# Rotary embedding on one core: from float16 halves on one software queue to float32 pieces on two hardware queues, with the additions on GpSimd

## The chip, the core and the metric

The kernel runs on one NeuronCore of a Trainium2 chip. A core has five instruction streams that matter here: TensorE (unused in this kernel), VectorE (DVE in the profile), ScalarE (ACT), GpSimd (POOL) and SyncE (SP). They run independently and meet through semaphores. SBUF is the on-chip working memory of 128 partitions, PSUM a second and smaller on-chip memory, and HBM the memory outside. Sixteen DMA engines move data between HBM and SBUF; an engine's queue (SP, ACT or POOL) issues a transfer, and the sixteen engines carry it out. A transfer issued by POOL appears in the profile as "software" queue, one issued by SP or ACT as "hardware" queue.

The metric is the device time of the program in microseconds, as the median of several runs. A profiled execution has its own time, and a span, which is the stretch that the trace covers.

## The reference

```python
def setup_inputs():
    batch, seq_len, num_heads, head_dim = (8, 2048, 16, 64)
    return {'x': ..., 'cos': ..., 'sin': ...}    # x [8, 2048, 16, 64], cos and sin [2048, 32], float32

def reference(x, cos, sin):
    x1 = x[..., :head_dim // 2]
    x2 = x[..., head_dim // 2:]
    out1 = x1 * cos - x2 * sin
    out2 = x1 * sin + x2 * cos
    return np.concatenate([out1, out2], axis=-1).astype(np.float32)
```

cos and sin are broadcast over the batch and the heads. The input is 67.1 MB and so is the output. For one element there are two products and one addition: the element times cos, the other half's element times sin (with a minus for the first half), and their sum.

## The kernel before

**Tiling.** The 2048 positions are spread over 128 partitions, so that each partition holds J = 16 consecutive positions ("rows" below); a row is 16 heads of 64 numbers, 1024 elements. One batch is thus a tile of 128 partitions by 16384 elements. All of it is computed in float16: the transfer that loads x converts from float32 to float16 on its way, the one that stores converts back.

**Memory.** `buf` holds five batches in float16 (`NBUF = 5`), batch b in slot b % 5. `v` is one temporary of a batch's size. The tables `cos_h` and `sin_h` are float16 in SBUF; `sin_h` holds minus sin for the first half of a head and sin for the second.

**Arithmetic.** `rotate` (L83 to L100) issues three VectorE instructions for a batch, or for some rows of it: L92 writes `v` as the swapped halves of x times `sin_h`; L98 multiplies `buf` by `cos_h` in place; L100 adds `v` into `buf`. The halves are swapped by reading with a negative step, at no extra instruction.

**Queues.** All large transfers, six loads (L71) and eight stores (L81), are issued by POOL. `in_ring` chains them so that POOL issues them in the order in which they are written. SP loads the tables (L40, L45) and the first two rows of the first batch as float32 (`head`, L41), which ACT converts (L106), and at the end SP stores the last two rows (L135), which ACT has converted back (L134). ACT also makes the float16 tables (L104, L105, L110).

**Order.** Loads of batches 0 and 1 are issued first; then the first two rows are rotated and a row of them is stored; loads of batches 2 to 4 follow; batches 0 to 2 are rotated and stored one by one; loads of batches 5 to 7 wait for the stores that free their slots; then batches 3 and 4, 5 and 6, and 7.

Of the kernel before, what the change touches and what calls it, by code (L numbers as in the profile page):

```python
# [1 line left out]

# [4 lines left out]


@with_exitstack  # L10
def kernel(
    ctx: ExitStack,
    tc: tile.TileContext,
    x: bass.AP,
    cos: bass.AP,
    sin: bass.AP,
    out: bass.AP,
):
    nc = tc.nc
    f16 = mybir.dt.float16  # L20
    f32 = mybir.dt.float32

    B, S, H, D = x.shape
    Dh = D // 2
    P = nc.NUM_PARTITIONS
    J = S // P
    NBUF = 5

    const_pool = ctx.enter_context(tc.tile_pool(name="rope_const", bufs=1))
    io_pool = ctx.enter_context(tc.tile_pool(name="rope_io", bufs=1))  # L30
    tmp_pool = ctx.enter_context(tc.tile_pool(name="rope_tmp", bufs=1))

    JA = 2
    head = const_pool.tile([P, JA, H, D], f32)
    x0 = x[0].rearrange("(p j) h d -> p j (h d)", j=J)
    sin_f = const_pool.tile([P, J, Dh], f32)
    cos_f = const_pool.tile([P, J, Dh], f32)
    cos_h = const_pool.tile([P, J, Dh], f16)
    sin_h = const_pool.tile([P, J, D], f16)
    nc.sync.dma_start(out=sin_f, in_=sin.rearrange("(p j) d -> p j d", j=J))  # L40
    nc.sync.dma_start(  # L41
        out=head.rearrange("p j h d -> p (j h d)"),
        in_=x0[:, 0:JA, :].rearrange("p j f -> p (j f)"),
    )
    nc.sync.dma_start(out=cos_f, in_=cos.rearrange("(p j) d -> p j d", j=J))  # L45

    buf = io_pool.tile([P, NBUF, J, H, D], f16)

    ring = []

    def in_ring(dma):
        if ring:
            tc.add_manual_dep(
                dma.ins,
                ring[-1].ins.name,
                mybir.DependencyInfo(mybir.DependencyClass.NoSync, mybir.DependencyReason.DATA),
                reason="order of the ring",
            )
        ring.append(dma)
        return dma  # L60

    def load(b, n=1):
        k = b % NBUF
        if n == 1:
            j0 = JA if b == 0 else 0
            dst = buf[:, k, j0:J, :, :].rearrange("p j h d -> p (j h d)")
            src = x[b].rearrange("(p j) h d -> p j (h d)", j=J)[:, j0:J, :].rearrange("p j f -> p (j f)")
        else:
            dst = buf[:, k : k + n, :, :, :].rearrange("p b j h d -> p b (j h d)")
            src = x[b : b + n].rearrange("b (p j) h d -> p b (j h d)", j=J)  # L70
        in_ring(nc.gpsimd.dma_start(out=dst, in_=src))  # L71

    def store(b, n=1, j0=0, j1=J):
        k = b % NBUF
        if n == 1:
            src = buf[:, k, j0:j1, :, :].rearrange("p j h d -> p (j h d)")
            dst = out[b].rearrange("(p j) h d -> p j (h d)", j=J)[:, j0:j1, :].rearrange("p j f -> p (j f)")
        else:
            src = buf[:, k : k + n, :, :, :].rearrange("p b j h d -> p b (j h d)")
            dst = out[b : b + n].rearrange("b (p j) h d -> p b (j h d)", j=J)  # L80
        return in_ring(nc.gpsimd.dma_start(out=dst, in_=src))  # L81

    def rotate(b, j0=0, j1=J):  # L83
        v = tmp_pool.tile([P, J, H, D], f16)
        n = j1 - j0
        js = slice(j0, j1)
        xt = buf[:, b % NBUF, js, :, :]
        shape = [P, n, H, 2, Dh]
        sin_b = sin_h[:, js, :].rearrange("p j (e d) -> p j e d", e=2).unsqueeze(2).to_broadcast(shape)
        cos_b = cos_h[:, js, :].unsqueeze(2).to_broadcast([P, n, 2 * H, Dh])  # L90
        xe = xt.rearrange("p j h (e d) -> p j h e d", e=2)
        nc.vector.tensor_mul(  # L92
            out=v[:, js, :, :].rearrange("p j h (e d) -> p j h e d", e=2),
            in0=xe[:, :, :, ::-1, :],
            in1=sin_b,
        )
        xw = xt.rearrange("p j h (e d) -> p j (h e) d", d=Dh)
        nc.vector.tensor_mul(out=xw, in0=xw, in1=cos_b)  # L98
        xa = xt.rearrange("p j h d -> p (j h d)")
        nc.vector.tensor_add(out=xa, in0=xa, in1=v[:, js, :, :].rearrange("p j h d -> p (j h d)"))  # L100

    load(0)
    load(1)
    nc.scalar.copy(out=sin_h[:, :, Dh:D], in_=sin_f)  # L104
    nc.scalar.mul(out=sin_h[:, :, 0:Dh], in_=sin_f, mul=-1.0)  # L105
    nc.scalar.copy(  # L106
        out=buf[:, 0, 0:JA, :, :].rearrange("p j h d -> p (j h d)"),
        in_=head.rearrange("p j h d -> p (j h d)"),
    )
    nc.scalar.copy(out=cos_h, in_=cos_f)  # L110
    rotate(0, 0, JA)
    store(0, 1, 0, 1)
    load(2, 2)
    load(4)
    rotate(0, JA, J)
    store(0, 1, 1, J)
    rotate(1)
    store(1)
    rotate(2)
    store(2)  # L120
    load(5, 2)
    load(7)
    rotate(3)
    rotate(4)
    store(3, 2)
    rotate(5)
    rotate(6)
    store(5, 2)
    rotate(7)
    gate = store(7, 1, 0, 9)  # L130
    store(7, 1, 9, J - JA)
    last = buf[:, 7 % NBUF, J - JA : J, :, :].rearrange("p j h d -> p (j h d)")
    dst = out[B - 1].rearrange("(p j) h d -> p j (h d)", j=J)[:, J - JA : J, :].rearrange("p j f -> p (j f)")
    nc.scalar.copy(out=head.rearrange("p j h d -> p (j h d)"), in_=last)  # L134
    end = nc.sync.dma_start(out=dst, in_=head.rearrange("p j h d -> p (j h d)"))  # L135
    tc.add_manual_dep(
        end.ins,
        gate.ins.name,
        mybir.DependencyInfo(mybir.DependencyClass.Sync, mybir.DependencyReason.DATA),
        reason="the last rows go out behind this part",  # L140
    )


# [1 line left out]
_INS = ['x', 'cos', 'sin']  # L145
_OUTS = [((8, 2048, 16, 64), 'float32')]


# [23 lines left out]
```

## Time and profile before

| what | value |
|---|---|
| median of 3 runs | 316.41 us (316.35 to 316.66) |
| the profiled execution | 316.6 us |
| its span | 314.8 us |
| VectorE busy | 209.1 us in 27 instructions |
| ScalarE busy | 6.8 us |
| GpSimd busy | 8.6 us, in 14 issues of transfers and 4 small memsets |
| HBM read, written | 67.63 MB, 67.11 MB |

The profiled execution takes 1.8 us more than its span. A line of the profile that names a tile or a source line gives, in this order, the line, the engine, the operation, output and inputs, the shapes, how many there were, the busy time in all and the mean of one in ns, and the idle time of that engine just before with what ended it. A line of the timeline begins with the start in us from the span's start, and the duration.

### The profile page before, as it was taken

To read this page: it belongs to the slowest core of one execution; us is meant where nothing else is said; L and a number is where in the kernel's file an instruction comes from. 1 tells how busy PE (TensorE), PEld (TensorE's weight loads), DVE (VectorE), ACT (ScalarE), POOL (GpSimd) and SP (SyncE) were. 2 spreads that over 40 slices of the span, in tenths; PEclk is the share of its full clock that TensorE was granted. 3 is DMA by queue.
4 is the path that set the end of the run, shared out by engine and by line. 5 is a ranking of instruction groups with operands and counts; after the bars stand their busy time and mean duration, and the time that the engine had idled before them with its cause. 6 is when DMAs were issued, how large, how long until landed. Compare 5 with 4: busy or idle time off the path is not lost.

```text
span 314.8 us, 115 instructions
## 1 busy us (share of the span) xinstructions
DVE 209.1 (66%) x27; ACT 6.8 (2%) x6; POOL 8.6 (3%) x18
## 2 busy tenths in 40 slices
DVE  0105999999499999999950000899999999910000
ACT  3200000000000000000000000000000000020000
POOL 1002000000000000000010000000000000010000
DMA  9899999999999899999999999999999999999998
GB/s 284 187 262 200 200 266 200 200 262 204 200 200 317 382 492 407 400 400 533 400 200 208 258 200 200 229 237 333 400 491 441 400 400 525 408 400 400 433 427 339
DMA packets 3104, 101.71 MB, mean 323 GB/s; under 512 B 288, under 2 KB 288, under 8 KB 672
## 3 DMA queue, kind: packets, MB, share of 16 engines
q0 software_dynamic: 2528, 99.09, 98.1%
q1 hardware_dynamic: 576, 2.62, 2.2%
HBM read 67.63 MB, written 67.11 MB: 428 GB/s over the span
## 4 chain that ended last, share of the span: by engine, by line
DVE 66%; another core or an unknown queue 13%; DMA 8%; ACT 1%; issue 0%; SPq 0%; DVEq 0%; ACTq 0%
DVE buf L98 22%; DVE buf L100 22%; DVE v L92 22%; DMA cos_f<-in_cos_dram 8%; ACT head L134 1%; ACT cos_h L110 0%; SPq L41 0%; SPq L40 0%; DVEq L92 0%; ACTq L134 0%
## 5 line engine op out<-in xcount | busy, mean ns | idle before, releaser
L92 DVE TENSOR_TENSOR v<-buf,sin_h 128x16384 f16<-128x16384 f16 (+2 forms) x9 | 69.7, 7744 | 51.4 <-DMA buf<-in_x_dram 41.2
L98 DVE TENSOR_TENSOR buf<-buf,cos_h 128x16384 f16<-128x16384 f16 (+2 forms) x9 | 69.7, 7744 | 15.8 <-ACT cos_h L110 15.5
L100 DVE TENSOR_TENSOR buf<-buf,v 128x16384 f16<-128x16384 f16 (+2 forms) x9 | 69.7, 7744 | 0.3
L81 POOL DMA_DIRECT2D out_dram<-buf x8 | 4.7, 586 | 219.4 <-DVE buf L100 219.4
L134 ACT CAST head<-buf 128x2048 f32<-128x2048 f16 x1 | 1.9, 1898 | 249.9 <-DVE buf L100 249.9
L71 POOL DMA_DIRECT2D buf<-in_x_dram x6 | 3.7, 628 | 49.7 <-DMA out_dram<-buf 48.9
L106 ACT CAST buf<-head 128x2048 f16<-128x2048 f32 x1 | 1.9, 1897 | 3.5 <-DMA head<-in_x_dram 3.5
L104 ACT ACT_TABLE_LOAD x1 | 1.3, 1283 | 0.7 <-PEq L156 0.7
L110 ACT CAST cos_h<-cos_f 128x512 f16<-128x512 f32 x1 | 0.6, 617 | 16.1 <-DMA cos_f<-in_cos_dram 16.1
L104 ACT CAST sin_h<-sin_f 128x512 f16<-128x512 f32 x1 | 0.6, 617 | 1.4 <-DMA sin_f<-in_sin_dram 1.4
L105 ACT ACTIVATE sin_h<-sin_f 128x512 f16<-128x512 f32 x1 | 0.6, 624 | 0.0
L156 POOL MEMSET const-float32-0.0<- 128x1 f32 x1 | 0.1, 100 | 0.2 <-issue 0.2
L156 POOL MEMSET const-bfloat16-1.0<- 128x1 bf16 x1 | 0.1, 103 | 0.0
L156 POOL MEMSET const-float32-1.0<- 128x1 f32 x1 | 0.1, 100 | 0.0
L156 POOL MEMSET const-uint8-127<- 128x1 uint8 x1 | 0.1, 100 | 0.0
## 6 DMA issues: line engine op xcount, KB each, us to landing
buf<-in_x_dram POOLq DMA_DIRECT2D x2, 8192.0 KB, 55.2
buf<-in_x_dram POOLq DMA_DIRECT2D x3, 4096.0 KB, 57.4
out_dram<-buf POOLq DMA_DIRECT2D x1, 7680.0 KB, 68.3
out_dram<-buf POOLq DMA_DIRECT2D x1, 4608.0 KB, 28.6
buf<-in_x_dram POOLq DMA_DIRECT2D x1, 3584.0 KB, 22.3
out_dram<-buf POOLq DMA_DIRECT2D x1, 2560.0 KB, 34.1
head<-in_x_dram SPq DMA_DIRECT2D x1, 1024.0 KB, 6.9
out_dram<-head SPq DMA_DIRECT2D x1, 1024.0 KB, 8.4
```

Of the source, the lines that this page charges most:

```text
L71: in_ring(nc.gpsimd.dma_start(out=dst, in_=src))
L81: return in_ring(nc.gpsimd.dma_start(out=dst, in_=src))
L92: nc.vector.tensor_mul(out=v[:, js, :, :].rearrange("p j h (e d) -> p j h e d", e=2), in0=xe[:, :, :, ::-1, :], in1=sin_b,)
L98: nc.vector.tensor_mul(out=xw, in0=xw, in1=cos_b)
L100: nc.vector.tensor_add(out=xa, in0=xa, in1=v[:, js, :, :].rearrange("p j h d -> p (j h d)"))
L104: nc.scalar.copy(out=sin_h[:, :, Dh:D], in_=sin_f)
L105: nc.scalar.mul(out=sin_h[:, :, 0:Dh], in_=sin_f, mul=-1.0)
L106: nc.scalar.copy(out=buf[:, 0, 0:JA, :, :].rearrange("p j h d -> p (j h d)"), in_=head.rearrange("p j h d -> p (j h d)"),)
L110: nc.scalar.copy(out=cos_h, in_=cos_f)
L134: nc.scalar.copy(out=head.rearrange("p j h d -> p (j h d)"), in_=last)
L156: nc = _bacc.Bacc("TRN2", target_bir_lowering=False, num_devices=1)
```

## The change

Nothing is float16 any more. The work is cut into sixteen pieces of eight rows, two for each batch, of 128 partitions by 8192 float32 elements (4 MB). `buf` has five slots of a piece.

- **Transfers.** SP issues every load (piece 0 in two parts, 2 and 6 rows), ACT every store (the last piece in three parts: rows 0 to 3, 4 and 5, 6 and 7). POOL issues none. The load of piece p + 5 waits for the store of piece p, which had its slot.
- **Tables.** ACT copies sin (with both signs) and cos into PSUM as float32.
- **Arithmetic.** A piece is rotated in two halves of four rows, 4096 elements each. For a half, VectorE makes `v` = swapped x times sin (L68) and `buf` = x times cos in place (L81); GpSimd adds `v` into `buf` (L87). `v` lies in a pool with two buffers of a half's size.
- **A row kept on VectorE.** In the second half of every odd piece one of the four rows has its sin product written to PSUM (`w`, L75), and VectorE adds it (L84), so that GpSimd adds three rows there. In the last piece, VectorE so adds one row of the first four, one of the next two and both of the last two.

```diff
-    buf = io_pool.tile([P, NBUF, J, H, D], f16)
+    tmp_pool = ctx.enter_context(tc.tile_pool(name="rope_tmp", bufs=2))
+    sin_p = ps_pool.tile([P, J, D], f32)
+    cos_p = ps_pool.tile([P, J, Dh], f32)
+    buf = io_pool.tile([P, NBUF, R, H, D], f32)
...
+    def load(p, r0=0, r1=R):
+        nc.sync.dma_start(out=flat(buf[:, p % NBUF, r0:r1, :, :]), in_=rows(x, p, r0, r1))
+
+    def store(p, r0=0, r1=R):
+        nc.scalar.dma_start(out=rows(out, p, r0, r1), in_=flat(buf[:, p % NBUF, r0:r1, :, :]))
+
+    def rotate(p, r0, r1, on_vector=0):
...
+        m = n - on_vector
+        if m:
+            v = tmp_pool.tile([P, C, H, D], f32)
+            nc.vector.tensor_mul(
+                out=v[:, 0:m, :, :].rearrange("p j h (e d) -> p j h e d", e=2),
+                in0=rev[:, 0:m, :, :, :],
+                in1=sin_b[:, 0:m, :, :, :],
             )
+        if on_vector:
+            w = psv_pool.tile([P, 2, H, D], f32)
+            nc.vector.tensor_mul(
+                out=w[:, 0:on_vector, :, :].rearrange("p j h (e d) -> p j h e d", e=2),
+                in0=rev[:, m:n, :, :, :],
+                in1=sin_b[:, m:n, :, :, :],
+            )
         xw = xt.rearrange("p j h (e d) -> p j (h e) d", d=Dh)
         nc.vector.tensor_mul(out=xw, in0=xw, in1=cos_b)
+        if on_vector:
+            xa = flat(xt[:, m:n, :, :])
+            nc.vector.tensor_add(out=xa, in0=xa, in1=flat(w[:, 0:on_vector, :, :]))
+        if m:
+            xa = flat(xt[:, 0:m, :, :])
+            nc.gpsimd.tensor_add(out=xa, in0=xa, in1=flat(v[:, 0:m, :, :]))
...
+    nc.sync.dma_start(out=sin_f, in_=sin.rearrange("(p j) d -> p j d", j=J))
+    load(0, 0, 2)
+    nc.sync.dma_start(out=cos_f, in_=cos.rearrange("(p j) d -> p j d", j=J))
+    load(0, 2, R)
+    for p in range(1, NBUF):
+        load(p)
...
+    for p in range(NP):
+        if p == 0:
+            rotate(p, 0, 2)
+            rotate(p, 2, 4)
+            rotate(p, 4, 8)
+            store(p)
+        elif p == NP - 1:
+            rotate(p, 0, 4, 1)
+            store(p, 0, 4)
+            rotate(p, 4, 6, 1)
+            store(p, 4, 6)
+            rotate(p, 6, 8, 2)
+            store(p, 6, 8)
+        else:
+            rotate(p, 0, 4)
+            rotate(p, 4, 8, p % 2)
+            store(p)
+        if p + NBUF < NP:
+            load(p + NBUF)
```

The order in which each engine gets its instructions is set by a scheduler when the program is built, and it is not the order of the text. From the second half of an even piece e to the second half of the next even piece, with o = e + 1, VectorE's stream in the built program reads as follows ("half 0" and "half 1" are a piece's first and second four rows):

```
L68 v  of piece e,   half 1   4096 elements   waits for the GpSimd addition of piece e-1, half 1
L68 v  of piece o,   half 0   4096            waits for the GpSimd addition of piece e,   half 0
L81 cos of piece e,  half 1   4096
L81 cos of piece o,  half 0   4096
L68 v  of piece o,   half 1   3072            waits for the GpSimd addition of piece e,   half 1
L75 w  of piece o,   half 1   1024
L68 v  of piece e+2, half 0   4096            waits for the GpSimd addition of piece o,   half 0
L81 cos of piece o,  half 1   4096
L81 cos of piece e+2, half 0  4096
L84 add of piece o,  half 1   1024
```

Each wait is there because `v` has two buffers: the addition before the last must have read its buffer before a new `v` is written. GpSimd has the additions alone, in the order of the halves, and each waits for the cos product of its half.

More of the change, by code (lines that the diff above doesn't have):

```diff
@@ L19 @@
     nc = tc.nc
-    f16 = mybir.dt.float16
     f32 = mybir.dt.float32
@@ L26 @@
     J = S // P
+    R = 8
+    C = 4
+    HALVES = J // R
+    NP = B * HALVES
     NBUF = 5
@@ L30 @@
     io_pool = ctx.enter_context(tc.tile_pool(name="rope_io", bufs=1))
[L31 to L35, printed above, removed]
+    tmp_pool = ctx.enter_context(tc.tile_pool(name="rope_tmp", bufs=2))
+    ps_pool = ctx.enter_context(tc.tile_pool(name="rope_ps", bufs=1, space=bass.MemoryType.PSUM))
+    psv_pool = ctx.enter_context(tc.tile_pool(name="rope_psv", bufs=1, space=bass.MemoryType.PSUM))
@@ L36 @@
     sin_f = const_pool.tile([P, J, Dh], f32)
     cos_f = const_pool.tile([P, J, Dh], f32)
[L38 to L45, printed above, removed]
-    buf = io_pool.tile([P, NBUF, J, H, D], f16)
@@ L49 @@
[L49 to L57, printed above, removed]
-            )
[L59 to L96, printed above, removed]
+    sin_p = ps_pool.tile([P, J, D], f32)
@@ new lines, with rows, flat @@
+    cos_p = ps_pool.tile([P, J, Dh], f32)
+    buf = io_pool.tile([P, NBUF, R, H, D], f32)
+    def rows(t, p, r0, r1):
+        b, j0 = p // HALVES, (p % HALVES) * R
+        return t[b].rearrange("(p j) h d -> p j (h d)", j=J)[:, j0 + r0 : j0 + r1, :].rearrange("p j f -> p (j f)")
+    def flat(t):
+        return t.rearrange("p j h d -> p (j h d)")
+    def load(p, r0=0, r1=R):
+        nc.sync.dma_start(out=flat(buf[:, p % NBUF, r0:r1, :, :]), in_=rows(x, p, r0, r1))
+    def store(p, r0=0, r1=R):
+        nc.scalar.dma_start(out=rows(out, p, r0, r1), in_=flat(buf[:, p % NBUF, r0:r1, :, :]))
@@ new lines, in rotate @@
+    def rotate(p, r0, r1, on_vector=0):
+        n = r1 - r0
+        j0 = (p % HALVES) * R + r0
+        js = slice(j0, j0 + n)
+        xt = buf[:, p % NBUF, r0:r1, :, :]
+        rev = xt.rearrange("p j h (e d) -> p j h e d", e=2)[:, :, :, ::-1, :]
+        sin_b = sin_p[:, js, :].rearrange("p j (e d) -> p j e d", e=2).unsqueeze(2).to_broadcast([P, n, H, 2, Dh])
+        cos_b = cos_p[:, js, :].unsqueeze(2).to_broadcast([P, n, 2 * H, Dh])
+        m = n - on_vector
[5 more added lines that the diff above has]
+                in1=sin_b[:, 0:m, :, :, :],
+            )
+        if on_vector:
[5 more added lines that the diff above has]
+            )
@@ L97, in rotate @@
         xw = xt.rearrange("p j h (e d) -> p j (h e) d", d=Dh)
         nc.vector.tensor_mul(out=xw, in0=xw, in1=cos_b)
[L99 to L141, printed above, removed]
+        if on_vector:
+            xa = flat(xt[:, m:n, :, :])
+            nc.vector.tensor_add(out=xa, in0=xa, in1=flat(w[:, 0:on_vector, :, :]))
@@ new lines, in rotate @@
+        if m:
[7 more added lines that the diff above has]
+        load(p)
+    nc.scalar.copy(out=sin_p[:, :, Dh:D], in_=sin_f)
+    nc.scalar.mul(out=sin_p[:, :, 0:Dh], in_=sin_f, mul=-1.0)
+    nc.scalar.copy(out=cos_p, in_=cos_f)
```

## The prediction

> **What bounds the kernel now.** I read the totals first, then the chain of waits, the groups by shape, two windows, the timeline, and the transfers' issues.
>
> ```profile
> span 314.8 us, 115 instructions
> DVE 209.1 (66%) x27; ACT 6.8 (2%) x6; POOL 8.6 (3%) x18
> DMA  9899999999999899999999999999999999999998
> ...
> q0 software_dynamic: 2528, 99.09, 98.1%
> q1 hardware_dynamic: 576, 2.62, 2.2%
> HBM read 67.63 MB, written 67.11 MB: 428 GB/s over the span
> ```
>
> VectorE is busy for two thirds of the span, the sixteen DMA engines for all of it: the DMA row shows no slice under 8 tenths. So the bound is the transfer of 134.74 MB. Two windows tell which side of a transfer sets its pace; their columns are the stretch, its length, the busy time of DVE, ACT and POOL, the TensorE clock, the DMA share, and GB/s on the destination's side:
>
> ```profile
> 26.00:52.00 26.00, 25.11 (x5) 0.62 (x1) 1.79 (x3) 1.00 1.01 222
> 277.00:305.00 28.00, 0.00 (x0) 1.56 (x1) 0.96 (x2) 1.00 1.01 431
> ```
>
> The first is nearly all loads, which land as float16: 222 GB/s there is 444 at the float32 source. The second is stores alone, 431 GB/s of float32. Both are full, so the float32 side sets the pace, at about 436 GB/s, and float32 from end to end will cost the DMA nothing more: 134.74 MB by 436 is 309 us.
>
> VectorE's own prices come from the groups by shape (the last numbers are busy us and mean ns of one):
>
> ```profile
> L92 DVE TENSOR_TENSOR v<-buf,sin_h 128x16384 f16<-128x16384 f16 x7 | 60.8, 8693 | 41.3 <-DMA buf<-in_x_dram 41.2
> L92 DVE TENSOR_TENSOR v<-buf,sin_h 128x2048 f16<-128x2048 f16 x1 | 1.2, 1226 | 10.0 <-ACT buf L106 10.0
> L106 ACT CAST buf<-head 128x2048 f16<-128x2048 f32 x1 | 1.9, 1897 | 3.5 <-DMA head<-in_x_dram 3.5
> L110 ACT CAST cos_h<-cos_f 128x512 f16<-128x512 f32 x1 | 0.6, 617 | 16.1 <-DMA cos_f<-in_cos_dram 16.1
> ```
>
> Between 2048 and 16384 elements VectorE takes 0.521 ns an element, plus 0.16 us fixed; ACT, by the same subtraction, 0.834 ns plus 0.19 us. The 41.2 us that VectorE waited for loads are the DMA bound seen from VectorE.
>
> **The change, part by part.**
>
> *Float32 on VectorE.* No row shows a float32 operation of two tensors. If only the count of elements mattered, the price stayed at 0.521 ns; if the bytes do, it doubles to 1.042. I take the double: two inputs and an output of twice the bytes through the same ports. An operation on 4096 elements is then 4.43 us, with the 0.02 us to the next one (the chain of waits shows that gap between VectorE's instructions) 4.45; 3072, 2048 and 1024 elements are 3.38, 2.31 and 1.25. The stream is 87 instructions on 273,408 elements (twice 131,072, and 11,264 for the rows that VectorE adds): 284.8 + 87 × 0.18 = 300.6 us. That is under the DMA's 309.
>
> *Additions on GpSimd.* 33 instructions, 119,808 elements. The trace has no GpSimd arithmetic at all. The nearest row is ACT's: one stream in, one out, 0.834 ns an element. An addition has two inputs; fed one after the other they take two such passes, 1.67 ns, and if the output takes its turn too, three, 2.50 ns. I take the middle, 2.09 ns, as an estimate, with ACT's 0.19 us fixed: P = 8.73 us for 4096 elements, Q = 6.60 for 3072, 256 us in all. One pass is the far end, and a rival below. The Trainium skill ("GPSIMD Engine Reference", section 3.1) gives 4497 ns for a float32 addition of 2048 elements and advises VectorE for such work; by that, an estimate, P would be 9.0, Q 6.75 and the time below 425; no trace here shows it.
>
> *The wait that this adds, and it decides.* By busy time alone all three would fit side by side: DMA 309, VectorE 301, GpSimd 256. But `v` has two buffers, and the built order puts the wait for a free one ahead of the cos product that GpSimd needs next. Follow one round, two pieces, from v of piece e half 1, at time 0, when GpSimd begins the addition of (e, half 0):
>
> - v of (o, half 0) cannot start before that addition ends, at P + 0.1. Behind it on VectorE stands cos of (e, half 1), for which GpSimd waits. So GpSimd idles for v and cos, 2 × 4.45.
> - GpSimd then does (e, half 1) and (o, half 0) back to back, 2P. Behind these VectorE has cos (o, half 0), v of 3072 and w, all covered; v of (e+2, half 0) waits for the second addition.
> - Again v and cos (o, half 1) run with GpSimd idle, 2 × 4.45; then the addition of 3072, Q; then the round begins anew.
>
> The round is 3P + Q + 4 × 4.45 and the hops between engines. One hop from VectorE to POOL is on the timeline:
>
> ```profile
> 28.01 1.22 DVE L100 TENSOR_TENSOR buf<-buf,v 128x2048 f16<-128x2048 f16 x1
> ...
> 29.53 0.54 POOL L81 DMA_DIRECT2D out_dram<-buf  x1 [27.08 <-DVE buf L100]
> ```
>
> It is 0.28 us; the way back I take as 0.1 (ACT starts 0.09 after the last L100). Two of each: 0.76. Round: 26.2 + 6.6 + 17.8 + 0.8 = 51.4 us, against 37 us of VectorE's work and 38.6 us of DMA (16.8 MB by 436). Half of the overlap that the change needs is lost in each round.
>
> *Start.* SP issues sin, two rows, cos and six rows, 4.72 MB: 0.74 to the first issue, 2.1 fixed (sin's 256 KB took 2.7 from issue to landing, 0.6 of it bytes) and 10.8 of bytes: the six rows land at 13.5. VectorE works on the first two rows meanwhile, and the writing of the PSUM tables (three ACT operations of 0.62) ends before them. Then v, v, cos, cos (2.31 + 4.45 + 2.31 + 4.45) to 27.0; piece 0's last addition (P + 0.4) to 36.1; v of 3072 and a cos to 44.0; P + 0.4 to 53.1; v, add, cos (10.15) to 63.2, where the first round begins.
>
> *Rounds and end.* Six rounds (pieces 2 to 13): 308.1, to 371.3. Then P + 0.1 (380.1), v of 3072 and cos (387.9), P + 0.4 (397.0), and the last piece on VectorE: three operations of 1.25, cos 2.31, an addition 1.25, then w, cos and addition of two rows, 6.93: 411.3. The last store of 1 MB: 2.1 fixed and 2.4 of bytes, 415.8.
>
> ```profile
> sin_f<-in_sin_dram SPq DMA_DIRECT2D x1, 256.0 KB, 2.7
> ```
>
> With the 1.8 us that the profiled execution has beyond its span (316.6 to 314.8; the median of the runs, 316.41, is 0.2 less), the forecast is **418 us**.
>
> *At no cost.* The transfers need 309 of 416 us, so whatever the hardware queues gain or lose lies under GpSimd's and VectorE's turns; were that cover gone, the DMA bound of about 316 would be back. The fourteen issues taken from POOL (8.4 us) and ACT's conversions were off the path. SP's loads wait for stores, which wait for additions: a piece stays in its slot for some 35 us of work, and five slots at 25.7 us each give 128. ACT's queue carries only stores by then, so a waiting store holds up only the next store.
>
> *Bounds.* At two passes (P 7.02, Q 5.32) the round is 44.9, start 59.8, and the sum 372; at three (10.44, 7.88) the round is 57.8 and the sum 463.
>
> **The rivals.**
>
> 1. *GpSimd is cheap* (not slower). If the addition takes one pass, 0.834 ns, P is 3.6, under VectorE's own 4.45, and no v waits. The point from which waiting decides is where the round equals VectorE's 37: P about 5.1, or 1.2 ns an element. Below it VectorE runs through: 13.5 less the 4.6 already done, plus 300.6, plus 4.5 for the store, plus 1.8: 315 to 316, and DMA's 309 with start and end gives the same. For it: ACT shows that a pass can be this quick. Against: that row has one input.
> 2. *Shared access*. GpSimd and VectorE shut each other out of SBUF, and the two work in turn: 8.9 + 300.6 + 256 + 6.3 = 572. For it: nothing in this trace, where GpSimd never computes. The Trainium skill ("SBUF — State Buffer", section "Who interferes with whom") says that they share a port pair, held for a whole instruction, but that a VectorE instruction with at most one SBUF input stays out of it; here the second input is always in PSUM. By that rule this rival falls; no run yet shows it.
> 3. *Float32 runs at float16's pace on VectorE*, 0.521 ns. Turns of 2.32 instead of 4.45 make the round 42.8, start 48, end 30 and 6.3: 342. Against: the same ports would have to carry twice the bytes.
> 4. *The change doesn't do what it says*: the engines overlap as meant and the built order does not hold VectorE. In the trace before, VectorE's instructions came in the built order, so I give this little; the time would be rival 1's.
>
> **How the numbers follow.** Forecast 0.80; rival 1 with 4 together 0.07; rival 2 0.07; rival 3 0.04; 0.02 for what I don't see. The range is the bounds of GpSimd's price, 372 to 463, which leaves out the rivals, 0.20. A difference of 0.2% (0.6 us) is about what this measurement tells from none. All but rival 1 are slower; there the time lies within 1 us of before: faster 0.04, same 0.01, slower 0.02 of its 0.07. Together faster 0.04, same 0.01, slower 0.95.
>
> **What will show it.** Right: VectorE idle for about 100 us, put down to GpSimd's additions and in front of L68; GpSimd idle for about 9 us before every second addition, released by L81; L87 at 8 to 9.5 us for 4096 elements; L68 and L81 at 4.4; DMA share near 75%. Wrong: additions of 4096 under 5 us and VectorE over 90% busy (rival 1), L68 and L81 stretched far over 4.4 beside an addition (rival 2), or near 2.3 (rival 3).

## The result, and the profile after

The changed kernel takes 417.9 us (median of 4 runs, 417.85 to 417.93) against 316.44 us before: a ratio of 1.3205, 95% interval 1.3182 to 1.3228. The forecast was 418, from 372 to 463. The profiled execution has a span of 416.1 us.

The totals, the DMA row and the queues of the changed kernel:

```profile
span 416.1 us, 295 instructions
DVE 294.1 (71%) x87; ACT 3.1 (1%) x4; POOL 258.8 (62%) x37
DMA  8999999899797987895877978787877409053198
...
q1 hardware_dynamic: 2736, 67.63, 39.9%
q10 hardware_dynamic: 2592, 67.11, 37.6%
HBM read 67.63 MB, written 67.11 MB: 324 GB/s over the span
```

No engine is full any more. VectorE is busy for 71% of the span, GpSimd for 62%, the DMA engines for 77.5% (the shares of the two queues, 39.9 and 37.6, together); in the kernel before, the DMA engines were full. Time that no engine fills is time in which the engines wait for one another. The list of waits of the changed kernel (who waited, for whom, us in total, times, longest) names them:

```profile
POOL buf L87 <- DVE buf L81: 143.9, 17, 10.5
DVE v L68 <- POOL buf L87: 104.4, 29, 4.7
DVE v L68 <- DMA buf<-in_x_dram: 9.3, 2, 6.2
```

VectorE waits 104.4 us for GpSimd, and GpSimd 143.9 us for VectorE: a ring of two engines, each waiting for the other by turns. Loads held VectorE up only twice, at the start. The groups by shape give the prices:

```profile
L87 POOL TENSOR_TENSOR buf<-buf,v 128x4096 f32<-128x4096 f32 x22 | 194.1, 8834 | 72.5 <-DVE buf L81 72.5
L81 DVE TENSOR_TENSOR buf<-buf,cos_p 128x4096 f32<-128x4096 f32 x30 | 131.5, 4415 | 0.1
L68 DVE TENSOR_TENSOR v<-buf,sin_p 128x4096 f32<-128x4096 f32 x22 | 97.3, 4421 | 64.3 <-POOL buf L87 64.3
L87 POOL TENSOR_TENSOR buf<-buf,v 128x3072 f32<-128x3072 f32 x8 | 53.5, 6694 | 53.5 <-DVE buf L81 53.5
L87 POOL TENSOR_TENSOR buf<-buf,v 128x2048 f32<-128x2048 f32 x2 | 9.0, 4516 | 18.0 <-DVE buf L81 18.0
```

Nearly all idle time stands in front of L68 on VectorE and in front of L87 on GpSimd; L81 never waits (0.1 us before thirty of them), because it stands behind an L68 that has done the waiting. One round, from the timeline of the two engines:

```profile
164.68 4.42 DVE L68 TENSOR_TENSOR v<-buf,sin_p 128x4096 f32<-128x4096 f32 x1 [1.41 <-POOL buf L87]
173.48 4.42 DVE L68 TENSOR_TENSOR v<-buf,sin_p 128x4096 f32<-128x4096 f32 x1 [4.37 <-POOL buf L87]
177.81 8.75 DVE L81 TENSOR_TENSOR buf<-buf,cos_p 128x4096 f32<-128x4096 f32 x2
182.37 17.63 POOL L87 TENSOR_TENSOR buf<-buf,v 128x4096 f32<-128x4096 f32 x2 [8.93 <-DVE buf L81]
191.25 3.35 DVE L68 TENSOR_TENSOR v<-buf,sin_p 128x3072 f32<-128x3072 f32 x1 [4.69 <-POOL buf L87]
...
200.03 4.42 DVE L68 TENSOR_TENSOR v<-buf,sin_p 128x4096 f32<-128x4096 f32 x1 [4.29 <-POOL buf L87]
204.37 8.74 DVE L81 TENSOR_TENSOR buf<-buf,cos_p 128x4096 f32<-128x4096 f32 x2
208.93 15.48 POOL L87 TENSOR_TENSOR buf<-buf,v 128x3072 f32<-128x3072 f32 x2 [8.93 <-DVE buf L81]
...
215.66 4.42 DVE L68 TENSOR_TENSOR v<-buf,sin_p 128x4096 f32<-128x4096 f32 x1 [1.41 <-POOL buf L87]
```

At 173.48 VectorE gets a free `v` and writes it; only then, from 177.81, comes the cos product for which GpSimd has been idle, and GpSimd starts at 182.37, after 8.93 us of nothing. It does two additions, and at 200.03 the same begins again. A round is 215.66 - 164.68 = 50.98 us, of which GpSimd works 33.11 and stands 2 × 8.93.

### The profile page after: what moved, and what is told of

The parts are those of the page before. It is cut to its first block, busy times and chain, and to the rows that moved or that the text cites. A ratio compares the mean times of both kernels' runs of the same rounds, so it can differ in the third digit from the quotient of the medians.

```text
span 416.1 us, 295 instructions
## 1 busy us (share of the span) xinstructions
DVE 294.1 (71%) x87; ACT 3.1 (1%) x4; POOL 258.8 (62%) x37
## 2 busy tenths in 40 slices
DMA packets 5330, 134.76 MB, mean 324 GB/s; under 512 B 592, under 2 KB 592, under 8 KB 848
## 3 DMA queue, kind: packets, MB, share of 16 engines
q1 hardware_dynamic: 2736, 67.63, 39.9%
q10 hardware_dynamic: 2592, 67.11, 37.6%
## 4 chain that ended last, share of the span: by engine, by line
POOL 46%; DVE 44%; issue 5%; DMA 3%; SPq 0%; POOLq 0%
POOL buf L87 46%; DVE buf L81 27%; DVE v L68 15%; DMA buf<-in_x_dram 3%; DVE buf L84 1%; DVE w L75 1%; SPq L52 0%; SPq L91 0%; POOLq L87 0%; SPq L89 0%
## 5 line engine op out<-in xcount | busy, mean ns | idle before, releaser
L87 POOL TENSOR_TENSOR buf<-buf,v 128x4096 f32<-128x4096 f32 (+3 forms) x33 | 258.6, 7857 | 143.9 <-DVE buf L81 143.9
L68 DVE TENSOR_TENSOR v<-buf,sin_p 128x4096 f32<-128x4096 f32 (+3 forms) x33 | 129.8, 3936 | 113.8 <-POOL buf L87 104.4
L81 DVE TENSOR_TENSOR buf<-buf,cos_p 128x4096 f32<-128x4096 f32 (+1 forms) x34 | 140.5, 4165 | 0.2
L75 DVE TENSOR_TENSOR w<-buf,sin_p 128x1024 f32<-128x1024 f32 (+1 forms) x10 | 13.3, 1330 | 0.1
L84 DVE TENSOR_TENSOR buf<-buf,w 128x1024 f32<-128x1024 f32 (+1 forms) x10 | 13.2, 1322 | 0.1
```

The costliest lines, as they stand in the source:

```text
L68: nc.vector.tensor_mul(out=v[:, 0:m, :, :].rearrange("p j h (e d) -> p j h e d", e=2), in0=rev[:, 0:m, :, :, :], in1=sin_b[:, 0:m, :, :, :],)
L75: nc.vector.tensor_mul(out=w[:, 0:on_vector, :, :].rearrange("p j h (e d) -> p j h e d", e=2), in0=rev[:, m:n, :, :, :], in1=sin_b[:, m:n, ...
L84: nc.vector.tensor_add(out=xa, in0=xa, in1=flat(w[:, 0:on_vector, :, :]))
L87: nc.gpsimd.tensor_add(out=xa, in0=xa, in1=flat(v[:, 0:m, :, :]))
```

## The experiments

Theory: the built order (v, v, cos, cos) and the two `v` buffers together lock the two engines in turns, at 3P + Q and four VectorE instructions a round. Rival A: the transfers, now on two hardware queues, set the pace. Rival B: GpSimd and VectorE disturb each other in SBUF. e1_cos_first was run four times and e6_no_row six times; every other time below is of one run.

**The order alone (e1_cos_first).** The cos product of a half is put ahead of the next half's v; every instruction and every wait that correctness needs stays.

```diff
+    behind = []
+
+    def in_turn(mul):
+        if behind:
+            tc.add_manual_dep(
+                mul.ins,
+                behind[-1].ins.name,
+                mybir.DependencyInfo(mybir.DependencyClass.NoSync, mybir.DependencyReason.DATA),
+                reason="cos of the half before goes first",
+            )
...
+            in_turn(mul)
...
-        nc.vector.tensor_mul(out=xw, in0=xw, in1=cos_b)
+        behind.append(nc.vector.tensor_mul(out=xw, in0=xw, in1=cos_b))
```

> The same kernel with one order imposed on VectorE: the cos product of a half goes ahead of the v of the next half. No wait is taken away and no size changes. Theory (built order and two v buffers lock GpSimd and VectorE in turns): a half is then v and cos, 8.86 us, and GpSimd's 8.83 fit beside it; VectorE runs through, 300 us of work from an effective start of 9 us, end of the span at 314 to 318, time 316 to 320, VectorE's wait for GpSimd under 10 us instead of 104. Rival A (the transfers on two hardware queues set the pace, 324 GB/s): no change, 416 to 420. Rival B (GpSimd and VectorE disturb each other in SBUF and the idle time is only where that shows): more overlap makes the instructions longer, L87 over 8.83 us or L68 and L81 over 4.42, and the time stays above 380.

Measured: 318.69 us, ratio to the kernel before 1.0075 (1.0058 to 1.0092). 99 of the 101 us are gone. The totals, the wait of v for GpSimd, and one group of e1_cos_first, whose lines have moved (L79 is v, L93 cos, L99 the GpSimd addition):

```profile
DVE 294.9 (93%) x87; ACT 3.1 (1%) x4; POOL 259.7 (82%) x37
...
DVE v L79 <- POOL buf L99: 1.8, 8, 0.3
...
L99 POOL TENSOR_TENSOR buf<-buf,v 128x4096 f32<-128x4096 f32 x22 | 194.6, 8862 | 28.4 <-issue 16.5 <-DVE buf L93 10.8 <-POOL buf L99 1.1
```

Both engines do the same work in nearly the same busy time; of the 104.4 us that VectorE waited for GpSimd, 1.8 are left. The additions, now beside VectorE nearly all the time, take 8862 ns instead of 8834. So rival A falls (the same transfers fit into 317 us), and so does rival B.

**Fewer slots, and a third buffer (e2_four_slots, e3_three_v).** Memory for a third `v` has to come from `buf`, so the control has four slots alone.

```diff
-    NBUF = 5
+    NBUF = 4
```

> Control for the next run: four slots of buf instead of five, nothing else; VectorE's order is unchanged. Theory: a slot is needed for about 50 to 60 us of load, turns and store, four rounds of half a 51 us round are 102, so 416 to 420 as before. Rival A (transfers): fewer slots leave fewer transfers in flight, so over 425.

Measured: 417.84 us, as the changed kernel. A slot less costs nothing there. Then, in addition:

```diff
-    tmp_pool = ctx.enter_context(tc.tile_pool(name="rope_tmp", bufs=2))
+    tmp_pool = ctx.enter_context(tc.tile_pool(name="rope_tmp", bufs=3))
```

> Four slots of buf, and three buffers of v instead of two (the freed slot makes room). VectorE's order keeps v, v, cos, cos. Theory: a v now waits for the addition three before, which has ended, so the turns are gone though the order stays: 325 to 332 by the same arithmetic (VectorE's 300 us, with the last additions ending later), wait of L68 for L87 under 20 us. If the order alone were the cause: about 418. Rival A: 418 or more.

Measured: 338.03 us. In the rounds VectorE's order is still v, v, cos, cos; at the start and near the end the scheduler moved a few instructions. The waits of e3_three_v:

```profile
DVE v L68 <- DMA buf<-in_x_dram: 31.7, 10, 7.7
...
DVE v L68 <- POOL buf L87: 0.5, 2, 0.3
```

The wait for GpSimd fell from 104.4 to 0.5 us: neither the order nor the two buffers lock the engines alone; it takes both. The time is 6 us over the range that was expected, and the new wait is for loads, 31.7 us.

**Four slots with the better order (e8_order_four).** The same cut of NBUF, on e1_cos_first.

> The order of e1_cos_first with four slots of buf instead of five; VectorE's order is the same. It tells whether the four slots alone explain why e3_three_v came out at 338 and not at 325 to 332: there L68 waited 31.7 us for loads, 22 more than elsewhere. If a slot less holds up the loads once the transfers are nearly full: 325 to 340, with waits of L79 for loads of 15 us and more. If it does not, 318 to 320, and e3_three_v's waits come from its order, in which a piece stays longer in its slot.

Measured: 324.15 us, with 17.8 us of waiting for loads; the range was missed by 1 us. So a missing slot costs 5.5 us once the transfers are full, where it cost nothing in the locked order. The other 14 us of e3_three_v are not explained by the slot. That its order keeps a piece longer in its slot is argued, not shown.

**Fewer bytes (e4_few_stores).**

```diff
     def store(p, r0=0, r1=R):
+        r1 = r0 + (r1 - r0 + 7) // 8
```

> The kernel with each store cut to an eighth of its rows: 59 MB of output are left out, everything else is the same. Theory: the transfers were covered, the rounds stay at 51 us and only the tail of the last store shortens: 413 to 418. Rival A (transfers set the pace): DMA work falls by 44%, and the time falls well below 380.

Measured: 413.57 us. VectorE's wait for GpSimd in e4_few_stores (L69 is v there, L88 the addition):

```profile
DVE v L69 <- POOL buf L88: 104.4, 29, 4.7
```

It is the same to a tenth; with 77.09 MB moved instead of 134.76 (58 MB less, where 59 was expected) only the tail behind the last addition shortened. The transfers were covered.

**Cheaper additions in the locked order (e10_three_quarters, e9_half_add).** The changed kernel, with GpSimd adding only a part of each half.

```diff
         if m:
-            xa = flat(xt[:, 0:m, :, :])
-            nc.gpsimd.tensor_add(out=xa, in0=xa, in1=flat(v[:, 0:m, :, :]))
+            h = m * H // 2
+            xa = flat(xt[:, 0:m, :, :])[:, 0 : h * D]
+            nc.gpsimd.tensor_add(out=xa, in0=xa, in1=flat(v[:, 0:m, :, :])[:, 0 : h * D])
```

(`h = m * H * 3 // 4` in the other.)

> The same with three quarters added: P 6.67, Q 5.05. Theory: the round is 20.0 + 5.1 + 18.5 = 43.6 against 51.0 in the changed kernel; six rounds and four additions of start and end less: 417.9 - 6 x 7.4 - 4 x 2.2 = 365, so 357 to 368, and a bend between this and the half. If the time followed GpSimd's busy time alone, 417.9 - 65 = 353 or, with the half at 288, no bend.

> The changed kernel with its built order and two v buffers, but GpSimd adds only the first half of what it added (the other half of those sums is left out). P is 4.5 us (the 2048 elements of the changed kernel took 4.52) and Q 3.4. Theory: the round by the formula, 3P + Q + 18.5 = 35.4, falls under VectorE's own 37, so the turns vanish though order and buffers are the same: 317 to 321, wait of L68 for GpSimd under 10 us. If the order cost its stalls whatever the price (a fixed price per wait): only GpSimd's own 130 us shrink, and 29 waits of 3.6 us stay, over 380.

Measured: 360.63 us for three quarters and 321.12 for the half, the latter 0.1 us over its range. L68's wait for GpSimd, first e10_three_quarters:

```profile
DVE v L68 <- POOL buf L88: 47.7, 22, 2.5
```

and e9_half_add:

```profile
DVE v L68 <- POOL buf L88: 2.7, 8, 0.4
```

The time falls by 57 us for the first quarter taken off GpSimd and by 40 for the second. It stops there because the transfers are full, and not only at VectorE's 37 us a round, as the expectation had it. A window in the middle of e9_half_add:

```profile
160.00:210.00 50.00, 47.69 (x14) 0.00 (x0) 23.95 (x6) 1.00 1.00 430
```

The DMA share is 1.00, VectorE is busy for 95%, and over the whole run it waits 15.8 us for loads.

The expectation made the first step worth 44 us in six rounds and 9 at the ends; it was 57. The round of e10_three_quarters took 42.89 us (from v at 193.60 to v at 236.49) where 43.6 was expected. The expectation put the two stretches in which GpSimd stands, with their hops, at 18.5 us; they are 2 × 8.93 = 17.86 in both kernels. So a round became 50.98 - 42.89 = 8.09 us shorter, and six rounds with the 9 at the ends make the 57. With P at 4.5 us, nearly one VectorE instruction, the same order and buffers make VectorE wait 2.7 us in all: the price of the addition decides whether the lock shows.

**No GpSimd at all (e7_no_gpsimd).**

```diff
-            nc.gpsimd.tensor_add(out=xa, in0=xa, in1=flat(v[:, 0:m, :, :]))
+            nc.vector.tensor_add(out=xa, in0=xa, in1=flat(v[:, 0:m, :, :]))
```

> The changed kernel with the additions of L87 moved to VectorE, GpSimd idle. Theory: 33 additions on 119,808 elements cost 1.042 ns an element and 0.18 fixed each, 130.7 us; with the 295 us that VectorE had that is 425, plus 9 of start and 6 of end: 436 to 446. So in the built order GpSimd hides only some 20 to 30 us of its 259. If the turns cost little and GpSimd hides most of its work, this should be over 500.

Measured: 432.27 us, 4 under the range. In the changed kernel GpSimd's 259 us of additions thus buy 14 us; in the better order they buy 114.

**Shared access, set up on purpose (e6_no_row, e5_tables_sbuf).** First the better order with all rows of the middle pieces on GpSimd:

```diff
-            rotate(p, 4, 8, p % 2)
+            rotate(p, 4, 8)
```

> The order of e1_cos_first, and GpSimd adds all rows of the pieces before the last: the seven w products and the seven VectorE additions of one row go. Theory: VectorE's work falls by 7 x (1.09 + 2 x 0.17) = 10 us to about 290, GpSimd's rises to 274, a half is 8.85 against 8.86 plus a hop of some 0.2; VectorE ends near 300 and the transfers are the limit, 309 us at 436 GB/s with about 4 us of start and end: span 312 to 315, time 313 to 317, at or just under the kernel before (316.4). If GpSimd's turn (8.86 and hops) set the pace instead: 32 x 9.3 plus 16, still under 315. If VectorE were not the limit of e1 but the transfers were: no gain, 318 to 319.

Measured: 318.78 us, ratio 1.0077 (1.0062 to 1.0092): no gain over e1_cos_first, though VectorE's work fell to 287.6 us and it ends at 304 instead of 308. The range was missed by 2 us. A window in the middle of e6_no_row, and its last 13 us, after VectorE's end (columns as in the prediction):

```profile
160.00:210.00 50.00, 49.22 (x12) 0.00 (x0) 49.33 (x7) 1.00 1.00 433
...
305.00:318.00 13.00, 0.00 (x0) 0.00 (x0) 0.00 (x0) 1.00 0.75 320
```

VectorE, GpSimd and the transfers are all full in the middle, and the DMA share is 1.00: the kernel is at the bound of the kernel before. So the last case of the expectation came out: e1_cos_first was held by the transfers already (a DMA share of 0.99 to 1.01 at 421 to 436 GB/s from 14 to 305 us), not by VectorE alone. 134.76 MB at 433 GB/s are 311 us, to which start and end add 6.5, not the 4 that were expected.

Then the tables in SBUF instead of PSUM, so that each product has two inputs in SBUF:

```diff
-    sin_p = ps_pool.tile([P, J, D], f32)
-    cos_p = ps_pool.tile([P, J, Dh], f32)
+    sin_p = const_pool.tile([P, J, D], f32)
+    cos_p = const_pool.tile([P, J, Dh], f32)
```

> As e6_no_row, but the tables lie in SBUF, not in PSUM, so both products have two SBUF inputs (the order is the same but for one w product of the last piece). This is the forecast's rival of shared access, set up on purpose. If GpSimd's addition and a VectorE product with two SBUF inputs shut each other out: VectorE's 290 and GpSimd's 274 stand one after the other, 560 to 590, with waits in front of, or longer rows for, L79, L93 or L99. If they don't: 313 to 318 as e6_no_row, and PSUM tables are worth nothing here.

Measured: 561.1 us. Three lines of the timeline of e5_tables_sbuf:

```profile
101.96 4.41 DVE L79 TENSOR_TENSOR v<-buf,sin_p 128x4096 f32<-128x4096 f32 x1
102.11 12.92 POOL L99 TENSOR_TENSOR buf<-buf,v 128x4096 f32<-128x4096 f32 x1 [4.36 <-DVE buf L93]
106.40 12.91 DVE L93 TENSOR_TENSOR buf<-buf,cos_p 128x4096 f32<-128x4096 f32 x1
```

The addition is issued while v runs and takes 12.92 us instead of 8.86, which fits one that stands until v ends. The cos product is issued at 106.40 and takes 12.91 instead of 4.42, which fits one that stands until the addition ends. A half is 17.3 us, nearly the sum of all three (4.42 + 4.42 + 8.83 is 17.7). By these lengths they shut each other out almost completely, and the profile shows this as busy time: VectorE reads 97% busy. This is the rule of the Trainium skill ("SBUF — State Buffer", section "Who interferes with whom") in both directions: with two SBUF inputs the engines take turns, 561 us; with one in PSUM they don't, 318.8.

## Why the prediction was right

*The bound before, and float32 on the DMA.* The float32 side sets a transfer's pace: right. e6_no_row moves float32 on both sides at 433 GB/s with a DMA share of 1.00, where 436 was taken.

*Float32 on VectorE.* 4.43 us was forecast for 4096 elements, 4.42 measured, with one input in PSUM; 4417 ns with both in SBUF (L87 in e7_no_gpsimd). Busy time 294.1 us against 300.6 with gaps. Where two instructions don't depend on each other, the second begins 0.09 us before the first ends (two L81 take 8.75), which the forecast had as a gap of 0.02.

*Additions on GpSimd.* This was the step with the least under it, between 1.67 and 2.50 ns an element; the middle, 2.09, met 2.11 (8834 less 4516, by 2048), and the fixed part of 0.19 met 0.20. P was 8.83 against 8.73, Q 6.69 against 6.60. Nothing in the trace before singled out the middle of two and three passes, so that it met is luck, and with it the closeness of 418 to 417.9; what the reasoning bore was the range, 372 to 463. No run shows that GpSimd works in passes. The Trainium skill's 4497 ns for 2048 elements ("GPSIMD Engine Reference", section 3.1) met 4516 here. Doubled to 9.0 us for 4096 elements, as the forecast did, it was 0.17 us too long, because a fixed part is in it.

*The wait.* Right in place, order and size, and shown by e1_cos_first and e3_three_v. The first round began at 62.7 (forecast 63.2), a round took 50.98 (51.4), and VectorE ended at 408.2 (411.3). VectorE's wait for GpSimd was given as about 100 us and is 104.4; GpSimd's before every second addition as about 9 and is 8.93. Inside the round two small errors worked against each other: v, cos and the hops were put at 18.6 us and are 17.86, the additions at 32.8 and are 33.1.

*The end.* Two errors cancelled, which is luck. The rounds were forecast 2.3 us too long in sum (and the start 0.5), and the last store was put at 4.5 us behind VectorE's end; it took 7.9 (8.2 from issue to landing, the median of the two stores of 1 MB). The trace before had a nearer row than the sum of fixed part and bytes: its last store of 1 MB (`out_dram<-head`) took 8.4 us from issue to landing.

*At no cost.* The cover of the transfers held: e4_few_stores takes 43% of the bytes away for 4 us of tail. And what was said of a gone cover came out with the better order: the bound of the transfers is back, at 318.8 in e6_no_row, where "about 316" was written.

*The rivals.* GpSimd cheap: not so, but its point of decision, P about 5.1, lies between e9_half_add (4.5, no lock) and e10_three_quarters (6.7, 48 us of waiting). The prediction's own round meets VectorE's 37 us at a P of about 4.9, so 5.1 is a little high; the runs can't tell the two apart. Shared access: absent here, and real as soon as the tables lie in SBUF; its forecast of 572 was 561 there, with a few rows split otherwise. Float16's pace on VectorE: not so (4.42 us, not 2.3). A scheduler that keeps to another order: not so, VectorE's instructions came in the built order.

## What to carry to other kernels

Busy times that fit side by side are no forecast: follow one round through the order that each engine really gets, and ask of every wait what stands behind it on that engine and who needs that. Here a wait for a buffer stood ahead of the one instruction that the other engine needed, and either a swap of two instructions (99 of 101 us) or one more buffer (80, with a slot less) gives most of it back. And where a kernel is at the bound of its transfers, as this one was, moving the arithmetic to other engines can at best come back to that bound: none of the versions run here beat the 316.4 us of the kernel before.

## What was not expected of the hardware

A VectorE instruction that is shut out of SBUF by GpSimd is shown as busy, not as waiting (12.91 us for a 4.42 us product). By that, nearly half of the 97% busy there was standing: the thirty cos products took 374.4 us, against 132.6 in e6_no_row. And the bounds of VectorE, GpSimd and the transfers can be met together: in the middle of e6_no_row all three are at 98% or more, with GpSimd's additions only 0.3% longer (8864 ns) than in the locked kernel.
